# Row sums in buffers of their own, and half of the down projection's sums added by DVE, in a two-layer encoder step

## The chip, the core and the metric

The kernel runs on one core of a Trainium2 chip. The metric is the device time of one execution in microseconds (us). The median of three runs of the kernel before is 2804.59 us (2801.84 to 2804.91). Five engines are spoken of: PE (the matrix engine), DVE (the vector engine), ACT (the scalar engine), POOL (GpSimd, used here mostly to start DMAs that add into their target) and SP (which starts the other DMAs). Each works through its own instructions in program order and waits at an instruction until its inputs and its output buffer are ready. SBUF is the on-chip memory that all of them read. PSUM holds eight banks of 128 x 512 fp32 into which PE writes its sums.

## The reference, cut to what matters

The computation is one inference step of two layers over 640 tokens (512 of a prompt, 128 of running streams). Each layer has a half-step feed-forward part, a mixer and a second half-step feed-forward part, each followed by a layer norm. The change touches the feed-forward parts alone:

```python
D_MODEL = 1024
D_FF = 2816

def swiglu(x, w_gate, w_up, w_down):
    return (jax.nn.silu(x @ w_gate) * (x @ w_up)) @ w_down
...
x = layer_norm(ALPHA * x + 0.5 * swiglu(x, ffn_w_gate[l, 0], ffn_w_up[l, 0], ffn_w_down[l, 0]),
               ln_g[l, 0], ln_b[l, 0])
```

All values are fp32. There are four feed-forward parts, ffn0 to ffn3, with the mixers between them in the order ffn0, mix0, ffn1, ffn2, mix1, ffn3.

## The kernel before, in words

**Precision.** PE multiplies in a reduced fp32 format, so every operand is held as two parts, hi and lo. `split(hi, lo, src)` makes them: ACT copies the source into hi (L94), which rounds it, and DVE subtracts hi from the source into lo (L95). A product of two operands is three matmuls (hi x hi, lo x hi, hi x lo). Weights come by DMA into a `raw` buffer (four of them, 128 x 1024), and their parts go into a `w` buffer (six of them). The last operand of a matrix has a single buffer of its own, `w1`.

**Gate and up.** The 2816 hid channels are 22 tiles of 128, taken two at a time (`pair`). For one pair, the gate and the up projection are each a 2 x 2 block product done with seven products in place of eight. `matrix` runs the seven products in the order 1, 2, 6, 5, 7, 3, 4 (12 matmuls each, L355), and `operands` prepares the seven weight operands: products 1 and 2 use the weight itself, 6 and 5 use two sums that DVE builds in a buffer `sw` (L334) and that are then split into `w`, 7 and 3 use differences that DVE writes over the raw weight, and 4 uses `w1`. There is one `sw` buffer. DVE joins the products into the hid row `hf` (L400, L404, L407), the gate through `s` (L392, and ACT's silu at L394); ACT keeps some products in `mx` (L366). The hid rows are split into `h`, the left operands of the down projection.

**The down projection.** Four hid tiles at a time (two pairs) are multiplied with their rows of w_down and added to the running sum `yacc` (five token tiles, 0 to 4, of 128 x 1024). In ffn0 and ffn3 this is plain. In ffn1 and ffn2 four of the six down projections of a part go through `down7`, which applies the seven-product scheme to token tiles 0 to 3 as well. It takes the token tiles in two pairs, `tp` = 0 (tiles 0 and 1) and `tp` = 1 (tiles 2 and 3); tile 4 is added plainly by DVE (L501). The scheme needs sums and differences of the hid tiles: `row_sums`, called after the up matrix of each pair, has DVE write four of them (L439 to L442) into the `sw` buffer and split them into `hs`. It needs sums and differences of the weights too, which DVE writes over the raw weights (L459 to L462) and splits into `w` buffers (called T in the code). Then come the products 1, 2, 5, 6, 3, 7, 4 (L485), each for both token pairs. After each, `add` puts the PSUM bank into `yacc`: ACT scales the bank into an `ev` buffer (L492; there are three, 128 x 512), and a DMA started by POOL adds the buffer to `yacc` (L493). The same bank is used again by a later product, so PE must wait until it has been read.

**Order.** The down projection of the four tiles before is issued inside the first pair of the next four, between the gate matrix and the preparation of the up operands. A scheduler of the framework then sets the order on each engine from the program order and from when buffers come free. So two pairs and one `down7` make a period that repeats: gate, down7, up, row sums, gate, up, row sums. There are eight `down7` (four each in ffn1 and ffn2), 16 row sums and 112 adds.

Of the kernel before, what the change touches and what calls it, by code (L numbers as in the profile page):

```python
# [9 lines left out]
F32 = mybir.dt.float32  # L10
# [3 lines left out]
ALU = mybir.AluOpType  # L14
# [3 lines left out]
ALPHA = 4.0 ** 0.25  # L18
# [17 lines left out]
def kernel(ctx: ExitStack, tc: tile.TileContext, I, O, phases=PHASES):  # L36
    nc = tc.nc

    def pool(name, bufs=1, stack=ctx, **kw):
        return stack.enter_context(tc.tile_pool(name=name, bufs=bufs, **kw))  # L40
# [24 lines left out]
    def bank_a():  # L65
        return bank("a")

    def bank_b():
        return bank("b")
# [23 lines left out]
    def split(hi, lo, src):  # L93
        nc.scalar.copy(hi, src)  # L94
        return nc.vector.tensor_tensor(lo, src, hi.bitcast(F32), op=ALU.subtract)  # L95

    def raw_tile():
        return pools["raw"].tile([128, 1024], F32, name="raw")
# [4 lines left out]
    def two_units():  # L103
        return pools["w"].tile([128, 2, 2, 512], F32R, name="w")

    def split2(w, src):

        return split(w[:, :, 0], w[:, :, 1], src.rearrange("p (j c) -> p j c", j=2))
# [19 lines left out]
    def mm3(ps, lhs, rhs):  # L128
        n = 3 * len(lhs)
        k = 0  # L130
        for (wh, wl), (xh, xl) in zip(lhs, rhs):
            for a, b in ((wh, xh), (wl, xh), (wh, xl)):
                state["pe"] = nc.tensor.matmul(ps, a, b, start=(k == 0), stop=(k == n - 1)).ins  # L133
                k += 1
# [3 lines left out]
    yacc = act.tile([128, NT, D], F32, name="yacc")  # L138
# [72 lines left out]
    def ffn(i, ph, last, side=None):  # L211


        V = nc.vector
        Q = T // 2
        with ExitStack() as st:
            wk = pool(f"ffn{i}_wk", 1, st, reuse_waits="tile")
# [45 lines left out]
            for h in range(2):  # L263
                o, L = HALVES[h]
# [12 lines left out]
            for r in range(2):  # L277
                w = load_w(I["w_gate"][i, 2 + r])
                first[r] = g_row()
                for c in range(2):  # L280
                    p = bank_a()[:, :Q]
# [102 lines left out]
            def pair(f, before=None):  # L384
# [26 lines left out]
                for n, take in (("w_gate", gate), ("w_up", up)):  # L411
                    if n == "w_gate" and f == 2:
                        tick("gate")
                        continue
                    if n == "w_up" and before is not None:
                        down(before)
                    with tc.issue_after(state["acc0"]) if f == 2 else ExitStack():
                        A = operands(I[n][i, f], I[n][i, f + 1])
                    if n == "w_up":
                        for r in range(2):  # L420
                            ht[f + r] = h_tile()
                    matrix(A, take)
                    if n == "w_up" and ph in SEVEN and f < NF - 4:
                        row_sums(f)
                    tick("gate" if n == "w_gate" else "up")

            def by_pairs(t):

                return t[:, :TP].rearrange("p (n a c) -> p n a c", n=2, a=2)
# [3 lines left out]
            def row_sums(f):  # L433


                v = wk.tile([128, 1024], F32, name="sw", bufs=1)
                s1, s2, s3, s4 = (v[:, 256 * n:256 * n + 256].rearrange("p (n c) -> p n c", n=2) for n in range(4))
                p, q = by_pairs(hf[f]), by_pairs(hf[f + 1])
                V.tensor_tensor(s1, p[:, :, 1], q[:, :, 1], op=ALU.add)  # L439
                V.tensor_tensor(s2, s1, p[:, :, 0], op=ALU.subtract)  # L440
                V.tensor_tensor(s3, p[:, :, 0], p[:, :, 1], op=ALU.subtract)
                V.tensor_tensor(s4, q[:, :, 0], s2, op=ALU.subtract)  # L442
                o = hs[f] = wk.tile([128, 2, 1024], F32R, name="hs", bufs=2)
                split(o[:, 0], o[:, 1], v)

            def down7(fs):


                raws, direct = {}, {}
                for f in fs:  # L450
                    raws[f] = raw_tile()
                    nc.sync.dma_start(raws[f], I["w_down"][i, f])
                for f in fs:
                    direct[f] = two_units()
                    split2(direct[f], raws[f])

                for f in fs[::2]:
                    (b11, b12), (b21, b22) = ((r[:, :512], r[:, 512:]) for r in (raws[f], raws[f + 1]))
                    V.tensor_tensor(b22, b22, b12, op=ALU.subtract)  # L459
                    V.tensor_tensor(b12, b12, b11, op=ALU.subtract)  # L460
                    V.tensor_tensor(b11, b22, b11, op=ALU.add)
                    V.tensor_tensor(b21, b21, b11, op=ALU.subtract)  # L462
                T = {}
                for r in range(2):
                    for f in fs[::2]:
                        T[f + r] = two_units()
                        split2(T[f + r], raws[f + r])

                def left(f, p, tp):
                    tok = lambda k, a: ht[f + k][:, :, 256 * tp + 128 * a:256 * tp + 128 * a + 128]  # L470
                    if p in (1, 2, 4):
                        return tok(*{1: (0, 0), 2: (1, 0), 4: (1, 1)}[p])
                    o = 256 * {5: 0, 6: 1, 7: 2, 3: 3}[p] + 128 * tp
                    return hs[f][:, :, o:o + 128]

                def right(f, p):
                    return {1: direct[f][:, 0], 2: direct[f + 1][:, 0], 3: direct[f + 1][:, 1],
                            6: T[f][:, 0], 5: T[f][:, 1], 4: T[f + 1][:, 0], 7: T[f + 1][:, 1]}[p]

                def product(ps, tp, p, first):  # L480
                    n = 0
                    for f in fs[::2]:
                        a, b = left(f, p, tp), right(f, p)
                        for u, v in ((0, 0), (1, 0), (0, 1)):
                            nc.tensor.matmul(ps, a[:, u], b[:, v], start=(first and n == 0), stop=(n == 5),  # L485
                                             skip_group_check=True)
                            n += 1

                def add(ps, t, j):

                    e = wk.tile([128, 512], F32, name="ev", bufs=3)
                    nc.scalar.mul(e, ps, 0.5 / ALPHA)  # L492
                    nc.gpsimd.dma_start(yacc[:, t, 512 * j:512 * j + 512], e, accum_op=ALU.add)  # L493

                t = NT - 1
                for j in range(2):
                    pb = bank_a()
                    mm3(pb, [(ht[f][:, 0, t * 128:t * 128 + 128], ht[f][:, 1, t * 128:t * 128 + 128]) for f in fs],
                        [(direct[f][:, j, 0], direct[f][:, j, 1]) for f in fs])
                    ya = yacc[:, t, j * 512:j * 512 + 512]  # L500
                    state["acc"] = V.scalar_tensor_tensor(ya, pb, 0.5 / ALPHA, ya, op0=ALU.mult, op1=ALU.add).ins  # L501
                x, w = ([bank_b() for _ in range(2)] for _ in range(2))
                z = [bank_a() for _ in range(2)]
                for p, ps, a, j in ((1, x, 0, 0), (2, z, 0, 0), (5, w, 1, 1), (6, x, 0, 1), (3, w, 0, 1), (7, x, 1, 1),
                                    (4, x, 1, 0)):
                    for tp in range(2):
                        product(ps[tp], tp, p, p in (1, 2, 5))
                        add(ps[tp], 2 * tp + a, j)
# [1151 lines left out]
```

## Time and profile before

| what | value |
|---|---|
| median of three runs | 2804.59 us (2801.84 to 2804.91) |
| profiled execution, its own time | 2807.14 us |
| its span, first to last instruction | 2805.4 us |
| mean granted PE clock | 0.965 |
| ACT casts of row sums (hs) | 16, 1045 ns each |
| adds through ev | 112 on ACT, 596 ns each; 112 DMAs of 256 KB |

Views of the profile used below: busy time of each engine in chosen stretches with the clock that PE was granted (1.00 is full speed); the list of waits, each as who waited for whom, total us, times, longest us; and timelines, which give start and duration in us, the engine, the line, the operation, and in brackets the idle time before it and what ended it. A timeline row marked x24 is 24 instructions of the same kind in a run, and its duration reaches to the end of the last one; PE's matmuls overlap a little, so the distance from one start to the next is the better measure of its pace. PEld is PE's loading of weights. Durations of grouped instructions are in ns.

### The profile page before, as it was taken

The page shows a single profiled execution, that of the slowest core. Times are in us where ns is not written, and L with a number is a line of the kernel's source. Part 1 is how long each engine was busy: PE and PEld are TensorE (multiplying, and loading weights), DVE is VectorE, ACT ScalarE, POOL GpSimd, SP SyncE. Part 2 cuts the span into 40 slices and gives each one's busy share as a digit, 9 for nine tenths or more (in the row PEclk, how much of TensorE's full clock was granted, in tenths as well). Part 3 has the DMA queues.
Part 4 walks back from the last instruction along what each step waited for, and adds up shares of the span by engine and source line. Part 5 has one row for each costly group of instructions (what it writes and reads, how often), then busy time and mean ns, then how long its engine had stood idle before and what let it go on. Part 6 is the DMA issues. An engine that isn't in the chain of part 4 may idle for free. (4 is left out here: it accounts for less than half of the span.)

```text
span 2805.4 us, 40790 instructions
## 1 busy us (share of the span) xinstructions
PE 2597.0 (93%) x15577; PEld 2335.0 (83%) x15577; DVE 2021.5 (72%) x3654; ACT 1247.7 (44%) x2372; POOL 336.5 (12%) x468
## 2 busy tenths in 40 slices
PE   8999999999798888889988888999999999999998
PEld 8999998786488777779878777888999978988887
DVE  7788876758577557467866557677768688876767
ACT  4344443346343444444344444456646453433332
POOL 0000003000020110113010110231111133000001
PEclk9999999999799999999999999999999999999999
DMA  5233344432211542553142552635646552344442
GB/s 175 91 118 106 106 133 136 154 122 66 79 46 59 114 116 63 123 120 113 44 103 72 128 113 76 159 104 178 207 131 198 177 183 74 103 144 131 139 137 91
DMA packets 181875, 332.12 MB, mean 118 GB/s; under 512 B 20864, under 2 KB 91648, under 8 KB 181168
## 3 DMA queue, kind: packets, MB, share of 16 engines
q1 hardware_dynamic: 163792, 293.83, 32.9%
q0 software_dynamic: 17888, 35.69, 6.7%
q8 instruction: 122, 2.00, 0.3%
q14 instruction: 73, 0.60, 0.1%
HBM read 259.56 MB, written 40.54 MB: 107 GB/s over the span
## 5 line engine op out<-in xcount | busy, mean ns | idle before, releaser
L95 DVE TENSOR_TENSOR w<-raw,w 128x512 fp32r<-128x512 f32 (+1 forms) x617 | 539.0, 896 | 238.5 <-ACT w L94 236.2
L94 ACT CAST w<-raw 128x512 fp32r<-128x512 f32 (+1 forms) x617 | 453.1, 771 | 312.3 <-PE bank L133 114.4
L133 PE MATMUL bank<-xhi,w 128*128 128x256 f32 (+2 forms) x2528 | 556.5, 312 | 15.8 <-ACT xhi L94 8.2
L355 PE MATMUL bank<-T,w 128*128 128x320 f32 x2736 | 467.1, 327 | 90.2 <-ACT w L94 82.2
L355 PE MATMUL bank<-xhi,w 128*128 128x320 f32 x2432 | 541.6, 310 | 0.2 <-DVE w L95 0.2
L355 PEld LDWEIGHTS bank<-T,w 128*128 128x128 f32 x2736 | 438.9, 202 | 102.5 <-ACT w L94 86.4
L133 PEld LDWEIGHTS bank<-xhi,w 128*128 128x128 f32 x2528 | 422.6, 189 | 28.1 <-ACT xhi L94 9.1
L133 PE MATMUL bank<-w,h 128*128 128x512 f32 x1872 | 436.7, 391 | 0.7 <-DVE w L95 0.7
L355 PEld LDWEIGHTS bank<-xhi,w 128*128 128x128 f32 x2432 | 408.5, 188 | 6.9 <-issue 4.2
L133 PEld LDWEIGHTS bank<-w,h 128*128 128x128 f32 x1872 | 348.1, 188 | 76.3 <-issue 3.4
L133 PE MATMUL bank<-xlo,w 128*128 128x256 f32 (+2 forms) x1264 | 391.7, 310 | 3.8 <-DVE xlo L95 3.6
L355 PE MATMUL bank<-xlo,w 128*128 128x320 f32 x1216 | 375.7, 309 | 0.0
L133 PEld LDWEIGHTS bank<-xlo,w 128*128 128x128 f32 x1264 | 238.4, 189 | 6.1 <-DVE xlo L95 4.7
L355 PEld LDWEIGHTS bank<-xlo,w 128*128 128x128 f32 x1216 | 228.9, 188 | 0.0
L493 POOL DMA_DIRECT2D yacc<-ev x112 | 97.1, 911 | 810.4 <-ACT ev L492 501.4
L366 ACT COPY mx<-bank 128x320 f32<-128x320 f32 x228 | 97.0, 425 | 180.7 <-PE bank L355 180.0
L208 DVE SCALAR_TENSOR_TENSOR yacc<-bank,yacc 128x512 f32<-128x512 f32 x160 | 109.6, 687 | 80.0 <-PE bank L133 79.2
L95 DVE TENSOR_TENSOR w<-sw,w 128x1024 fp32r<-128x1024 f32 x76 | 93.0, 1223 | 60.7 <-ACT w L94 60.3
L400 DVE TENSOR_TENSOR hf<-bank,mx 128x320 f32<-128x320 f32 x120 | 58.6, 488 | 106.0 <-PE bank L355 100.7
L94 ACT CAST w<-sw 128x1024 fp32r<-128x1024 f32 x76 | 79.6, 1048 | 107.4 <-DVE sw L334 106.7
L492 ACT ACTIVATE ev<-bank 128x512 f32<-128x512 f32 x112 | 65.9, 596 | 129.7 <-DMA yacc<-ev 103.3
L485 PE MATMUL bank<-w,hs 128*128 128x512 f32 x384 | 96.3, 403 | 22.1 <-ACT ev L492 22.1
(415 smaller groups left out, 3351.6 us busy)
## 6 DMA issues: line engine op xcount, KB each, us to landing
raw<-in_w_gate_dram SPq DMA_DIRECT2D x88, 512.0 KB, 4.1
raw<-in_w_up_dram SPq DMA_DIRECT2D x88, 512.0 KB, 4.5
raw<-in_w_down_dram SPq DMA_DIRECT2D x88, 512.0 KB, 3.7
yacc<-ev POOLq DMA_DIRECT2D x112, 256.0 KB, 4.5
raw<-in_m_in_dram SPq DMA_DIRECT2D x52, 512.0 KB, 4.5
raw<-in_m_out_dram SPq DMA_DIRECT2D x24, 512.0 KB, 4.0
csb<-cs_d SPq DMA_DIRECT2D x20, 512.0 KB, 4.9
h<-in_ssd_h_dram SPq DMA_DIRECT2D x16, 512.0 KB, 5.9
```

Of the source, the lines that this page charges most:

```text
L94: nc.scalar.copy(hi, src)
L95: return nc.vector.tensor_tensor(lo, src, hi.bitcast(F32), op=ALU.subtract)
L133: state["pe"] = nc.tensor.matmul(ps, a, b, start=(k == 0), stop=(k == n - 1)).ins
L208: state["acc"] = nc.vector.scalar_tensor_tensor(ya, pb, scale, ya, op0=ALU.mult, op1=ALU.add).ins
L355: nc.tensor.matmul(ps, A[p][:, a, k * 128:k * 128 + 128], B[p][b][:, k, :], start=(first and n == 0), stop=(n == 11), skip_group_check=True)
L366: nc.scalar.copy(e[n], ps)
L400: V.tensor_tensor(t[:, c], ps, e, op=ALU.add)
L485: nc.tensor.matmul(ps, a[:, u], b[:, v], start=(first and n == 0), stop=(n == 5), skip_group_check=True)
L492: nc.scalar.mul(e, ps, 0.5 / ALPHA)
L493: nc.gpsimd.dma_start(yacc[:, t, 512 * j:512 * j + 512], e, accum_op=ALU.add)
```

## The change

Two edits are made. `row_sums` takes two `ev` buffers of 512 columns in place of the one `sw` buffer of 1024, and so splits them in two halves. In `down7`, `add` of token tiles 2 and 3 (`t // 2` is 1, the second token pair) is one DVE instruction from the PSUM bank to `yacc`; tiles 0 and 1 keep ACT, ev and the DMA. No buffer is added: `sw` stays for `operands` alone, and the three `ev` buffers serve both users.

```diff
             def row_sums(f):
 
 
-                v = wk.tile([128, 1024], F32, name="sw", bufs=1)
-                s1, s2, s3, s4 = (v[:, 256 * n:256 * n + 256].rearrange("p (n c) -> p n c", n=2) for n in range(4))
+                v = [wk.tile([128, 512], F32, name="ev", bufs=3) for _ in range(2)]
+                s1, s2, s3, s4 = (v[n // 2][:, n % 2 * 256:n % 2 * 256 + 256].rearrange("p (n c) -> p n c", n=2)
+                                  for n in range(4))
                 p, q = by_pairs(hf[f]), by_pairs(hf[f + 1])
...
                 o = hs[f] = wk.tile([128, 2, 1024], F32R, name="hs", bufs=2)
-                split(o[:, 0], o[:, 1], v)
+                for n in range(2):
+                    split(o[:, 0, 512 * n:512 * n + 512], o[:, 1, 512 * n:512 * n + 512], v[n])
...
                 def add(ps, t, j):
 
+                    if t // 2:
+                        ya = yacc[:, t, j * 512:j * 512 + 512]
+                        V.scalar_tensor_tensor(ya, ps, 0.5 / ALPHA, ya, op0=ALU.mult, op1=ALU.add)
+                        return
                     e = wk.tile([128, 512], F32, name="ev", bufs=3)
                     nc.scalar.mul(e, ps, 0.5 / ALPHA)
                     nc.gpsimd.dma_start(yacc[:, t, 512 * j:512 * j + 512], e, accum_op=ALU.add)
```

The scheduler answers with another order on DVE and ACT in ffn1 and ffn2; the parts outside these two keep theirs, as do POOL and SP but for the 56 DMAs that go. The first place is DVE's queue in ffn1 at the end of the up matrix of hid tiles 6 and 7 and the start of the gate matrix of tiles 8 and 9. Before, `sw` holds the row sums first and then the sums for the gate's products 6 and 5:

```order
L95 TENSOR_TENSOR h<-hf,h 128x640
L439 TENSOR_TENSOR sw<-hf 128x256
L95 TENSOR_TENSOR w_8976<-raw,w_8976 128x512
L95 TENSOR_TENSOR h<-hf,h 128x640
L440 TENSOR_TENSOR sw<-sw,hf 128x256
L442 TENSOR_TENSOR sw<-hf,sw 128x256
L392 TENSOR_TENSOR s<-bank,mx 128x320
L95 TENSOR_TENSOR hs<-sw,hs 128x1024
L334 TENSOR_TENSOR sw<-raw 128x512
L334 TENSOR_TENSOR sw<-sw,raw 128x512
L95 TENSOR_TENSOR w<-sw,w 128x2x512
```

After the change (lines past the first edit have moved by one) the gate's sums come at the start of the stretch, among the joins of the hid rows:

```order
L334 TENSOR_TENSOR sw<-raw 128x512
L400 TENSOR_TENSOR hf<-bank,mx 128x320
L334 TENSOR_TENSOR sw<-sw,raw 128x512
L95 TENSOR_TENSOR w<-sw,w 128x2x512
L334 TENSOR_TENSOR raw<-raw,sw 128x512
L334 TENSOR_TENSOR raw<-raw 128x512
L400 TENSOR_TENSOR hf<-bank,mx 128x320
```

The row sums come after eight other rows of the same queue, now in ev:

```order
L440 TENSOR_TENSOR ev<-hf 128x256
L442 TENSOR_TENSOR ev<-hf 128x256
L441 TENSOR_TENSOR ev<-ev,hf 128x256
L392 TENSOR_TENSOR s<-bank,mx 128x320
L443 TENSOR_TENSOR ev<-hf,ev 128x256
L95 TENSOR_TENSOR hs<-ev,hs 128x512
```

The sums for the gate's operands and their split stand ahead of the hid rows (hf) and the row sums, where they stood behind both. The second place is DVE's queue during the `down7` just before, from the plain adds of token tile 4 to the preparation of the up operands. Before:

```order
L501 SCALAR_TENSOR_TENSOR yacc<-bank,yacc 128x512 x2
L95 TENSOR_TENSOR w<-raw,w 128x2x512 x2
L95 TENSOR_TENSOR w_8840<-raw,w_8840 128x512
L95 TENSOR_TENSOR w<-raw,w 128x2x512
L334 TENSOR_TENSOR sw<-raw 128x512
L334 TENSOR_TENSOR sw<-sw,raw 128x512
L95 TENSOR_TENSOR w<-sw,w 128x2x512
L334 TENSOR_TENSOR raw<-raw,sw 128x512
L334 TENSOR_TENSOR raw<-raw 128x512
```

After (L495 is the new add on DVE, L507 the plain add that was L501):

```order
L507 SCALAR_TENSOR_TENSOR yacc<-bank,yacc 128x512 x2
L495 SCALAR_TENSOR_TENSOR yacc<-bank,yacc 128x512
L95 TENSOR_TENSOR w<-raw,w 128x2x512 x2
L495 SCALAR_TENSOR_TENSOR yacc<-bank,yacc 128x512
L95 TENSOR_TENSOR w_8832<-raw,w_8832 128x512
L495 SCALAR_TENSOR_TENSOR yacc<-bank,yacc 128x512 x2
L95 TENSOR_TENSOR w<-raw,w 128x2x512
L334 TENSOR_TENSOR sw<-raw 128x512
L334 TENSOR_TENSOR sw<-sw,raw 128x512
L495 SCALAR_TENSOR_TENSOR yacc<-bank,yacc 128x512
L95 TENSOR_TENSOR w<-sw,w 128x2x512
L334 TENSOR_TENSOR raw<-raw,sw 128x512
```

The adds stand between the splits of the difference weights (the first x2), the split of `w1` and the up operands. The sixth and the seventh add follow further down, each behind one more difference of the raw weight.

## The prediction

> **What bounds the kernel now.** I read the page first, then busy time and clock by stretches, then the waits, then the timelines around the two longest waits of the tensor engine (PE).
>
> ```profile
> PE 2597.0 (93%) x15577; PEld 2335.0 (83%) x15577; DVE 2021.5 (72%) x3654; ACT 1247.7 (44%) x2372; POOL 336.5 (12%) x468
> PE   8999999999798888889988888999999999999998
> PEclk9999999999799999999999999999999999999999
> ```
>
> PE is the bound overall, but its busy row dips in the middle slices, where ffn1 and ffn2 run. The stretches show more. The first six rows of this view are whole periods of ffn1 and ffn2 (two pairs of hid tiles and one seven-product down projection each, cut at the same point of the program); the last is a stretch of ffn0, which has neither row sums nor seven-product down projections.
>
> ```profile
> 945.20:1044.20 99.00, 82.17 (x444) 74.67 (x444) 60.12 (x83) 43.32 (x64) 12.16 (x15) 0.91 0.42 102
> ...
> 1667.60:1766.60 99.00, 82.85 (x444) 74.94 (x444) 60.03 (x83) 43.35 (x64) 12.10 (x15) 0.91 0.41 101
> sum 595.60, PE 494.08 PEld 447.81 DVE 360.09 ACT 259.57 POOL 72.73; mean PE 82.35 PEld 74.64 DVE 60.01 ACT 43.26 POOL 12.12
> 100.00:200.00 100.00, 99.42 (x589) 92.54 (x588) 85.39 (x211) 40.54 (x70) 6.77 (x3) 1.00 0.33 108
> ```
>
> The columns are PE, PEld, DVE, ACT, POOL, the granted clock and the DMA share. A period takes 595.6/6 = 99.3 us, with PE busy 82 us of it at a clock of 0.91; in ffn0 PE is busy 99.42 of 100 us at 1.00, beside a DVE that is busy 85.39. So PE loses time in ffn1 and ffn2. The waits say to whom:
>
> ```profile
> PE bank L355 <- ACT w L94: 82.2, 16, 5.2
> PE bank L485 <- ACT ev L492: 46.2, 26, 3.0
> ACT ev L492 <- DMA yacc<-ev: 103.3, 63, 5.6
> DVE w L95 <- ACT w L94: 296.5, 200, 11.6
> ```
>
> Sixteen waits of 5.1 us come after the sixteen row sums. One of them on PE, with the clean products before it:
>
> ```profile
> 949.50 0.45 PE L355 MATMUL bank<-xhi,w 128*128 128x320 f32 x2
> ...
> 953.01 3.74 PE L355 MATMUL bank<-T,w 128*128 128x320 f32 x24
> 956.59 0.45 PE L355 MATMUL bank<-xhi,w 128*128 128x320 f32 x2
> ...
> 961.86 0.46 PE L355 MATMUL bank<-xhi,w 128*128 128x320 f32 x2
> ...
> 970.67 0.90 PE L355 MATMUL bank<-T,w 128*128 128x320 f32 x2 [5.13 <-ACT w L94]
> 971.93 5.16 PE L355 MATMUL bank<-T,w 128*128 128x320 f32 x22 [0.36 <-DVE w L95]
> ...
> 976.93 0.45 PE L355 MATMUL bank<-xhi,w 128*128 128x320 f32 x2
> ```
>
> A matrix of seven products (84 matmuls) takes 961.86 - 949.50 = 12.36 us when nothing waits. At 961.86 the gate matrix of the next pair begins; after two products it needs the operand that is split from sw. That comes late, because sw still holds the row sums:
>
> ```profile
> 965.33 0.43 DVE L442 TENSOR_TENSOR sw<-hf,sw 128x256 f32<-128x256 f32 x1
> 966.87 1.23 DVE L95 TENSOR_TENSOR hs<-sw,hs 128x1024 fp32r<-128x1024 f32 x1 [0.71 <-ACT hs L94]
> 968.13 0.69 DVE L334 TENSOR_TENSOR sw<-raw 128x512 f32<-128x512 f32 x1
> 968.85 0.69 DVE L334 TENSOR_TENSOR sw<-sw,raw 128x512 f32<-128x512 f32 x1
> 969.58 1.04 ACT L94 CAST w<-sw 128x1024 fp32r<-128x1024 f32 x1 [2.37 <-DVE sw L334]
> 970.65 1.23 DVE L95 TENSOR_TENSOR w<-sw,w 128x1024 fp32r<-128x1024 f32 x1 [1.11 <-ACT w L94]
> ```
>
> The wait costs more than its length. The 24 matmuls after it span 970.67 to 976.93, 6.26 us, where the clean 24 from 953.01 to 956.59 took 3.58: 0.36 of the difference is a second wait, 2.3 us is a slower array. The clock rows show it:
>
> ```profile
> 955.00:965.00 10.00, 10.00 (x70) 10.00 (x70) 5.61 (x11) 3.16 (x6) 0.00 (x0) 1.00 0.17 32
> 970.60:974.00 3.40, 2.97 (x10) 2.57 (x11) 2.43 (x3) 0.90 (x2) 0.00 (x0) 0.50 0.00 0
> 977.00:983.00 6.00, 6.00 (x43) 6.00 (x42) 4.17 (x7) 3.02 (x6) 0.00 (x0) 1.00 0.21 77
> ```
>
> So one row sum costs 5.13 + 0.36 + 2.3 = 7.8 us. The other place is the down projection:
>
> ```profile
> 916.53 5.63 PE L133 MATMUL bank<-w,h 128*128 128x512 f32 x24
> 922.00 5.60 PE L485 MATMUL bank<-w,h 128*128 128x512 f32 x24
> 927.43 5.60 PE L485 MATMUL bank<-w,hs 128*128 128x512 f32 x24
> 935.21 3.05 PE L485 MATMUL bank<-w,hs 128*128 128x512 f32 x12 [2.17 <-ACT ev L492]
> 939.12 3.18 PE L485 MATMUL bank<-w,hs 128*128 128x512 f32 x12 [0.86 <-ACT ev L492]
> 945.20 4.45 PE L485 MATMUL bank<-w,h 128*128 128x512 f32 x12 [2.91 <-ACT ev L492]
> ```
>
> Clean, 24 matmuls of 512 columns take 927.43 - 916.53 = 10.90 us for 48, so 5.45. A product for one pair of token tiles (6 matmuls) is 1.36 us. Three waits of 5.9 us together are for ACT, which waits for a free ev buffer.
>
> **The change part by part.** *What PE needs without any wait.* A period is four matrices and 108 matmuls of 512 columns: 4 x 12.36 + 108/24 x 5.45 = 49.4 + 24.5 = 73.9 us. It takes 99.3, so 25.4 us per period are waits and slow clock. ffn1 and ffn2 have eight periods (112 adds of 14 each; 16 row sums at two each): 8 x 25.4 = 203 us. Row sums are 16 x 7.8 = 125 of that; the remaining 78 go to the eight down projections and smaller pieces.
>
> *Row sums in ev buffers.* The sums for the next gate matrix no longer wait for the row sums; the first fence on the order shows them issued ahead of the whole hid chain. The operand that came at 970.65 is then built during the up matrix. Removed: 125 us. Added: the split of hs in two halves. From the row of 1.23 us for 1024 columns and 0.69 for 512 (968.13, the same kind of two-operand instruction), that is 2 x 0.69 - 1.23 = 0.15 us of DVE a time, 0.3 per period, beside PE. Added too: s1 to s4 now wait until the accumulating DMAs have freed two ev buffers. Behind that wait on DVE stand the hs split and the splits of the next weights.
>
> ```profile
> L492 ACT ACTIVATE ev<-bank x112: 582/597/602, 923.6 to 1773.3; 128x512 f32<-128x512 f32 x112
> L493 POOL DMA_DIRECT2D yacc<-ev x112: 852/859/1226, 924.5 to 1774.1; - x112
> ...
> DMA to landing us min/median/max: 3.3/4.5/8.0
> ```
>
> ```profile
> L501 DVE SCALAR_TENSOR_TENSOR yacc<-bank,yacc x16: 679/683/689, 923.0 to 1746.0; 128x512 f32<-128x512 f32 x16
> ```
>
> The last DMA of a down projection is issued at its end, and the row sums come a 12.36 us matrix later. Even the slowest landing of 8.0 us is over by then, so I cost this wait at nothing; without that cover it is at most 8.0 us once per period.
>
> *Adds on DVE.* Seven of fourteen adds per down projection leave ACT (0.60 us each), POOL's queue (0.86) and the DMA. An ev buffer is held for 0.60 + 0.86 + 4.5 = 6.0 us, so three buffers let one add through every 2.0 us, while PE finishes a product every 1.36: that is the wait of today. With every second product on ACT they come every 2.7 us, and the ev wait goes. DVE gets 7 x 0.68 = 4.8 us per period. (The nearest row is the same instruction at L501.) DVE needs 60.0 + 4.8 + 0.3 = 65.1 us in a period of 73.9, which is 88%; ffn0 shows 85.39% beside a PE at 99.42. An exact 85.39% limit would make the period 76.2, 2.3 us more. That is the upper end for this cost; the lower is zero.
>
> *What is late next.* An add on DVE waits for its product on PE, and behind it in DVE's queue stand the splits of the difference weights (for products 7 and 4) and the operands of the next up matrix. I count from PE's first matmul of the down projection (t = 0): tile 4 to 5.45, then two token pairs of 1.36 us for each of products 1, 2, 5, 6, 3, 7, 4, so their ends are 8.2, 10.9, 13.6, 16.4, 19.1, 21.8 and 24.5. The splits for products 7 and 4 need weight buffers that product 1 frees at 8.2: a cast of 1.04 and two splits of 1.23 end at 11.7, and product 7 starts at 19.1. The up operands need buffers that product 6 frees at 16.4: cast and split 18.7, two differences 20.1, the add of product 3 20.8, the split from sw (cast ready at 21.1) 22.4; the up matrix wants it after two products, at 24.5 + 24/84 x 12.36 = 28.0. The tightest place is the last product: after one more difference (23.1) DVE adds product 7's second pair, which ends at 23.8, and PE wants that bank at 21.8 + 1.36 = 23.2. So PE may wait 0.6 us there, too little to slow the array much: the 12 matmuls behind the 0.86 us wait above took 3.18 us.
>
> *The sum.* Between 0 and 2.4 us per period stay; I take 1.2, half of the DVE limit, since both the count and the ffn0 row are nearer to no wait. Span 2805.4 - 203 + 10 = 2612. The profiled execution took 2807.1 and the median of the runs is 2804.6, 0.8 below the span, so the forecast is 2612.
>
> The 2.3 us of slow clock per wait and the shorter ones after the down projections are 25.4 minus the waits themselves (82.2 + 16 x 0.36 + 46.2 = 134 us, 16.8 per period), some 8.6 us per period, 69 us in all. The Trainium skill ("TensorE: Matmul & The Clock Gate", What's actually happening) says that an idle window of about 3.4 us halves the array's clock, with which the 0.50 above agrees, but also "For modeling, the ramp penalty is <1% of a typical kernel span". By that rule no more than 28 us of the 203 could be ramp, the gain would be 134 + 28 = 162, and the time 2653; the rows here say 2.5% of the span, and I go by them.
>
> **The rivals.**
> 1. *DVE becomes the bound.* For it: 88% busy in program order, and 1.11 us of waiting for ACT's cast at each split like the one at 970.65. Two of these in each of four matrices (8.9 us) and half a product (0.7 us) at each of seven adds (4.9) on top of 65.1 make 78.9 us per period, 5 more than PE: 40 us back, 2642. Against it: the new order puts other work into most of these gaps.
> 2. *The down projections still wait,* for DVE in place of ACT; only the row sums' 125 us go: 2680. For it: the adds stand among splits that wait for ACT. Against it: the margins counted above.
> 3. *The row sums' wait stays,* because the gate's operands now wait for something else, such as a weight buffer: 78 us go, 2727. Against it: the gate's buffers come free when the gate before is done.
> 4. *Slower.* DVE falls behind through the adds, and PE waits at the sw operand of all four matrices of a period as it does today at two, each at 7.8 us: 31.2 in place of 25.4, 46 us more, 2851. It decides once DVE needs more than today's 99.3 us per period; it needs 65.1 now.
> 5. *It does nothing,* as the row sums and adds were covered: about 2805. Against it: PE's wait rows name exactly ev and the operand from sw.
>
> **How the numbers follow.** My forecast has 0.70, rivals 1 to 5 have 0.10, 0.10, 0.05, 0.03 and 0.02. The forecast alone spans 2602 to 2621 (0 to 2.4 us per period). The range takes in rival 1 and a half-kept wait in the down projections (39 us over 2621): 2598 to 2660, with 0.5 us per period below for the reading of the clean period. Faster by over 0.2% (5.6 us, about what a measurement of this kernel tells from no change): 0.95; within: 0.02; slower: 0.03.
>
> **What would show it.** In the profile after, the sixteen 5 us waits of PE L355 for ACT's cast should be gone, the ev wait for DMA nearly so, PE at 98% or more and the clock at 0.99 or more in ffn1 and ffn2, and the period 74 to 76 us. I am wrong if PE waits there for DVE's adds, if DVE is over 95% busy in a period, or if 5 us waits stay.

## The result and the profile after

The changed kernel takes 2602.9 us (median of four runs, 2601.0 to 2604.5) against 2804.75 (four runs): a ratio of 0.9281, 95% interval 0.9265 to 0.9297. That is 202 us less, 197 to 206. The forecast was 2612 and its range 2598 to 2660.

Page of the changed kernel, the same rows as of before:

```profile
PE 2532.5 (97%) x15577; PEld 2294.5 (88%) x15577; DVE 2037.3 (78%) x3726; ACT 1214.9 (47%) x2332; POOL 285.8 (11%) x412
...
PE   9999999999969999999999999999999999999998
PEclk9999999999979999999999999999999999999999
```

The dip in the slices of ffn1 and ffn2 is gone; the one that is left (the twelfth slice, 716 to 781 us) lies in the mixer ahead of ffn1, outside the change. Two whole periods of ffn1, cut at the plain adds of token tile 4 (columns as in the prediction: PE, PEld, DVE, ACT, POOL, granted clock, DMA share):

```profile
908.62:982.39 73.77, 73.77 (x445) 69.27 (x444) 62.44 (x92) 39.13 (x59) 6.15 (x7) 1.00 0.41 111
982.39:1056.20 73.81, 73.81 (x445) 69.31 (x444) 62.17 (x92) 39.15 (x59) 6.06 (x7) 1.00 0.42 111
```

A period is 73.8 us where it was 99.3, PE is busy in all of it, and its clock is 1.00. The waits that answer to the four of before:

```profile
ACT ev L498 <- PE bank L487: 76.2, 40, 3.0
...
PE bank L355 <- ACT mx L366: 0.8, 3, 0.4
...
PEld bank L487 <- DVE yacc L495: 1.5, 8, 0.2
...
DVE w L95 <- ACT w L94: 141.5, 129, 7.1
```

The sixteen 5 us waits of PE's L355 for ACT's cast are gone: the row shown is the one that L355 has left in the list for PE's matmuls, and its longest wait is 0.4 us. ACT now waits for PE's products and no longer for a free ev buffer. No wait of PE's matmuls in the down projection is in the list. The only trace of the new adds on PE is 0.2 us of its weight load, once per down projection. DVE's own waits for ACT's casts, which rival 1 feared, have halved (296.5 us before).

The first place of the change, the end of the up matrix and the start of the next gate matrix (timeline; DVE and PE rows):

```profile
931.31 0.68 DVE L334 TENSOR_TENSOR sw<-sw,raw 128x512 f32<-128x512 f32 x1
932.03 1.05 ACT L94 CAST w<-sw 128x1024 fp32r<-128x1024 f32 x1 [2.56 <-DVE sw L334]
...
933.11 1.23 DVE L95 TENSOR_TENSOR w<-sw,w 128x1024 fp32r<-128x1024 f32 x1 [1.12 <-ACT w L94]
...
942.92 3.68 PE L355 MATMUL bank<-T,w 128*128 128x320 f32 x24
...
944.37 0.41 DVE L443 TENSOR_TENSOR ev<-hf,ev 128x256 f32<-128x256 f32 x1
944.74 0.69 DVE L95 TENSOR_TENSOR hs<-ev,hs 128x512 fp32r<-128x512 f32 x1
```

The operand from sw is split at 933.11 and done at 934.3. PE wants it at 942.92, 8.6 us later, and the row sums are still being written then. Before, PE stood at this point, and the same split came behind the row sums. The 24 matmuls take 3.68 us here.

The second place, the end of the down projection:

```profile
913.34 11.04 PE L487 MATMUL bank<-w,hs 128*128 128x512 f32 x48
924.22 1.52 PE L487 MATMUL bank<-w,h 128*128 128x512 f32 x6
925.73 1.67 PE L487 MATMUL bank<-w,h 128*128 128x512 f32 x6
```

Four products for both token pairs run without a break, and the last follows; before, three waits stood among these.

### The profile page after: what moved, and what is told of

The parts are those of the page before. It is cut to its first block, busy times and chain, and to the rows that moved or that the text cites. A ratio compares the mean times of both kernels' runs of the same rounds, so it can differ in the third digit from the quotient of the medians.

```text
span 2602.8 us, 40675 instructions
## 1 busy us (share of the span) xinstructions
PE 2532.5 (97%) x15577; PEld 2294.5 (88%) x15577; DVE 2037.3 (78%) x3726; ACT 1214.9 (47%) x2332; POOL 285.8 (11%) x412
## 5 line engine op out<-in xcount | busy, mean ns | idle before, releaser
L355 PE MATMUL bank<-xhi,w 128*128 128x320 f32 x2432 | 541.9, 310 | 0.7 <-ACT mx L366 0.4
L355 PE MATMUL bank<-T,w 128*128 128x320 f32 x2736 | 425.9, 309 | 0.4 <-ACT mx L366 0.4
L355 PEld LDWEIGHTS bank<-xhi,w 128*128 128x128 f32 x2432 | 406.0, 188 | 8.3 <-issue 4.4
L355 PEld LDWEIGHTS bank<-T,w 128*128 128x128 f32 x2736 | 406.3, 188 | 1.7 <-ACT mx L366 0.6
L355 PE MATMUL bank<-xlo,w 128*128 128x320 f32 x1216 | 375.0, 308 | 0.0
L355 PEld LDWEIGHTS bank<-xlo,w 128*128 128x128 f32 x1216 | 228.0, 188 | 0.3
L499 POOL DMA_DIRECT2D yacc<-ev x56 | 48.6, 902 | 652.1 <-ACT ev L498 597.9
L133 PE MATMUL bank<-w,og 128*128 128x512 f32 x432 | 106.3, 400 | 2.8 <-DVE og L1460 2.8
L133 PEld LDWEIGHTS bank<-w,og 128*128 128x128 f32 x432 | 80.6, 191 | 21.1 <-DVE og L1460 4.6
L394 ACT ACTIVATE s<-s 128x320 f32<-128x320 f32 x108 | 50.8, 471 | 88.4 <-DVE s L392 88.2
```

What stands on the lines that cost most here:

```text
L355: nc.tensor.matmul(ps, A[p][:, a, k * 128:k * 128 + 128], B[p][b][:, k, :], start=(first and n == 0), stop=(n == 11), skip_group_check=True)
L394: state["silu"] = nc.scalar.activation(t, ps, AF.Silu).ins
```

## The experiments

Each run is given as its ratio to the kernel before on the same chip, and as us on the scale of 2804.6.

**Row sums alone.** The edit of `row_sums` without that of `add`:

```diff
-                v = wk.tile([128, 1024], F32, name="sw", bufs=1)
+                v = [wk.tile([128, 512], F32, name="ev", bufs=3) for _ in range(2)]
...
-                split(o[:, 0], o[:, 1], v)
+                for n in range(2):
+                    split(o[:, 0, 512 * n:512 * n + 512], o[:, 1, 512 * n:512 * n + 512], v[n])
```

> Only the row sums move into two ev buffers; all fourteen adds of a down projection stay with ACT and the DMA. If the two edits remove two separate waits, as the prediction has it, the sixteen row-sum waits go at 7.8 us each (wait and slow clock) and the down projections keep theirs: 2805 - 125 = 2680 us. If the slow clock is worth little (a ramp under 1% of the span), a wait is worth its idle time of 5.5 us: 2805 - 88 = 2717 us or a little less. If one cause lies behind both kinds of wait, this edit alone gives either all (2603 us) or nothing (2805 us).

Ratio 0.9524 (0.9500 to 0.9547): 2671 us, 133 less (127 to 140). Two periods, and the two waits that stay:

```profile
929.41:1012.45 83.04, 77.95 (x445) 71.27 (x445) 58.91 (x85) 42.66 (x66) 12.16 (x15) 0.96 0.50 121
1012.45:1095.45 83.00, 77.06 (x444) 70.07 (x444) 58.68 (x85) 42.56 (x66) 12.16 (x15) 0.98 0.50 120
```

```profile
ACT ev L494 <- DMA yacc<-ev: 108.4, 62, 7.5
...
PE bank L487 <- ACT ev L494: 44.8, 26, 3.5
```

The list of PE's waits has no more L355 for ACT's cast of w, while the wait for ev is nearly as before (46.2). A period is 83.0 us: one down projection costs 83.0 - 73.8 = 9.2 us of waiting and slow clock.

**Adds alone.** The edit of `add` without that of `row_sums`:

```diff
                 def add(ps, t, j):
 
+                    if t // 2:
+                        ya = yacc[:, t, j * 512:j * 512 + 512]
+                        V.scalar_tensor_tensor(ya, ps, 0.5 / ALPHA, ya, op0=ALU.mult, op1=ALU.add)
+                        return
```

> Only the adds of token tiles 2 and 3 move to DVE; the row sums stay in sw. Two separate waits: the down projections' share of 78 us goes, 2727 us, and with the other edit alone the two savings add up to the whole of 202 us. Slow clock worth little: 46 us of idle time and some pieces, about 2755 us. One common cause: 2603 or 2805 us.

Ratio 0.9747 (0.9723 to 0.9771): 2734 us, 71 less (64 to 78). With the other edit that makes 204 us, against 202 for both at once, where each of the two savings is good to 7 us. So these are two separate waits, and the savings add.

```profile
964.31:1054.49 90.18, 79.20 (x444) 73.45 (x445) 64.17 (x90) 39.39 (x57) 6.09 (x7) 0.92 0.35 91
1054.49:1145.22 90.73, 79.74 (x445) 73.99 (x445) 64.24 (x90) 39.58 (x57) 6.06 (x7) 0.93 0.34 90
```

```profile
964.31 0.90 PE L355 MATMUL bank<-T,w 128*128 128x320 f32 x2 [5.13 <-ACT w L94]
965.57 5.87 PE L355 MATMUL bank<-T,w 128*128 128x320 f32 x22 [0.36 <-DVE w L95]
```

The 5.13 us wait is as it was, and the 22 matmuls behind it stay slow: 5.87 us, where the sixteen rows of the kernel before run from 4.58 to 6.04. A period is 90.5 us, so two row sums cost 16.7, or some 8.3 each.

**No accumulating DMA.** The DMAs behind the scaled ev buffers are left out, and with them the sums of token tiles 0 to 3:

```diff
                     e = wk.tile([128, 512], F32, name="ev", bufs=3)
                     nc.scalar.mul(e, ps, 0.5 / ALPHA)
-                    nc.gpsimd.dma_start(yacc[:, t, 512 * j:512 * j + 512], e, accum_op=ALU.add)
```

> The kernel before without the DMA behind each scaled ev buffer: the down projection's sums of token tiles 0 to 3 are scaled by ACT but never added to yacc (this part of the computation is left out). DVE gets no extra work and ACT keeps all of its own. If the buffers that the accumulating DMAs hold are the whole of the down projections' wait, this is as fast as the kernel with only the adds moved: 2727 us, and the DVE adds are free. If ACT's own work or queue is part of that wait, it stays above, towards 2805 us; if the DVE adds cost something, it comes out below the kernel with only the adds moved.

Ratio 0.9744 (0.9718 to 0.9771), 2733 us (2726 to 2741): the kernel with only the adds moved, to within 1 us. All 112 scalings stay on ACT here and DVE has nothing more to do. So what made PE wait was the time that the DMAs held the ev buffers, neither ACT's work nor its queue, and the seven DVE adds per down projection cost nothing that these runs can tell. More ev buffers, the other way to shorten that wait, were not tried.

**More work on PE.** Thirty needless matmuls in the wait behind the row sums (`warm` is set for the sixteen gate matrices that follow row sums):

```diff
                 take(0, 0, z, e[1])
+                if warm:
+                    d = bank_b()[:, :Q]
+                    for n in range(30):
+                        nc.tensor.matmul(d, A[2][:, 0, n % 4 * 128:n % 4 * 128 + 128], B[2][0][:, n % 4, :],
+                                         start=(n == 0), stop=(n == 29), skip_group_check=True)
                 product(x, A, 6, False)
```

> The kernel before with 30 needless matmuls of 320 columns (4.4 us) put on PE at each of the sixteen gate matrices that follow row sums, between its second and third product, into a PSUM bank that nobody reads. The wait for the operand from sw stays as long as it was, but PE is busy for most of it. If the array slows because PE stands idle, the 2.3 us of slow matmuls behind each wait go: 2805 - 16 x 2.3 = 2768 us, faster with more work. If the ramp is worth under 1% or the matmuls behind the wait are slow for another reason (DVE or DMA using the same memory), the time stays at 2805 us or rises.

Ratio 0.9915 (0.9891 to 0.9939): 24 us less (17 to 31) with 480 more matmuls. The place that was at 970.67 before:

```profile
961.93 0.46 PE L355 MATMUL bank<-xhi,w 128*128 128x320 f32 x2
...
965.45 4.56 PE L376 MATMUL bank<-xhi,w 128*128 128x320 f32 x30
970.75 0.56 PE L355 MATMUL bank<-T,w 128*128 128x320 f32 x2 [0.74 <-ACT w L94]
972.01 3.49 PE L355 MATMUL bank<-T,w 128*128 128x320 f32 x22 [0.70 <-DVE w L95]
975.33 0.64 PE L355 MATMUL bank<-xhi,w 128*128 128x320 f32 x2
```

```profile
970.70:974.00 3.30, 2.55 (x15) 2.29 (x16) 2.43 (x3) 0.81 (x1) 0.00 (x0) 1.00 0.00 0
```

```profile
PE bank L490 <- ACT ev L497: 49.7, 25, 3.4
```

Counted from the start of the gate matrix, the operand comes as late as before (8.8 us: 970.75 - 961.93, and 970.67 - 961.86), and the clock is 1.00 where it was 0.50. So the matmuls were slow because PE had stood idle.

It gives less than the 37 us expected, first because not all of the 2.3 us was slow clock. The first two of the 24 matmuls start 1.26 us ahead of the other 22 at each of the sixteen places, in both kernels, where two clean ones take 0.30 (3.58 / 12): they wait for the lo part that DVE makes, whatever the clock, and that wait costs 0.96 us and not 0.36. Only the 22 behind can gain. At this place they go from 5.00 us (976.93 - 971.93) to 3.32 (975.33 - 972.01), 1.7 less; over the sixteen places their rows fall from a mean of 5.35 us to 3.49, which makes 30 us. Second, the waits for ev in the down projections are 49.7 us where they were 46.2. That leaves 26 us, and 24 came.

**All adds on DVE.**

```diff
-                    if t // 2:
+                    if True:
```

> The changed kernel with all fourteen adds of a down projection on DVE, so that ACT, ev and the DMA have none. DVE was busy 62.3 of 73.8 us in a period of the changed kernel; seven more adds at 0.60 us from start to start make it 66.5, 90%. If PE stays the bound as long as DVE has any room, the time is the changed kernel's, 2603 us within 0.2%. If DVE must stay near the 85% that ffn0 shows, a period grows to 66.5 / 0.854 = 77.9 us, 4.1 more, and the kernel to 2636 us.

Ratio 0.9286 (0.9266 to 0.9307), 2604 us: no difference from the changed kernel (0.9281) that these runs can tell.

```profile
905.90:979.87 73.97, 73.79 (x445) 69.33 (x444) 66.70 (x100) 34.64 (x52) 0.00 (x0) 1.00 0.27 86
979.87:1054.04 74.17, 74.06 (x446) 69.56 (x445) 66.77 (x99) 34.66 (x52) 0.00 (x0) 1.00 0.27 86
```

DVE is busy 66.7 of 74.1 us, 90%, and PE still loses at most 0.4 us per period. DVE has no limit at 85% here.

**DVE overloaded.** One needless instruction behind each of these adds, then two (in the second expectation, "the kernel before" is the kernel with one):

```diff
                         V.scalar_tensor_tensor(ya, ps, 0.5 / ALPHA, ya, op0=ALU.mult, op1=ALU.add)
+                        V.tensor_tensor(ya, ya, ya, op=ALU.max)
```

> All adds on DVE, and behind each one needless instruction on DVE (the maximum of the sum with itself, 128 x 512, about 0.60 us from start to start). DVE then needs 66.5 + 8.4 = 74.9 us in a period, 101% of PE's 73.8. If PE's work sets the time until DVE is full, the least is 1.1 us per period, 9 us in all: 2612 us or a little over. If DVE's order costs PE waits that slow its clock, as the rival of a DVE bound has it, each matrix may lose some us: 1.1 + 4 x 2 us per period, about 2675 us.

> As the kernel before, with two needless instructions behind each add: DVE needs 83.3 us in a period against PE's 73.8. DVE must be the bound now: at least 9.5 us per period more, 76 us, 2679 us. With waits for ACT's casts (1.1 us at each of eight splits per period) and half a product at each of fourteen adds it would be nearer to 2679 + 8 x 18 = 2820 us. If DVE's time in a period is not what counts, it stays at 2603 us.

Ratios 0.9462 (0.9441 to 0.9483), 2654 us, and 0.9712 (0.9693 to 0.9732), 2724 us. Both lie between the least that DVE's busy time asks for and the dearer expectation. A period of each, the first with one instruction, the second with two:

```profile
1006.64:1085.88 79.24, 75.68 (x444) 69.33 (x444) 74.75 (x113) 35.00 (x52) 0.00 (x0) 1.00 0.25 80
```

```profile
1019.91:1108.63 88.72, 80.41 (x444) 72.69 (x444) 83.13 (x127) 35.06 (x52) 0.00 (x0) 0.94 0.23 72
```

And the waits of PE in the second:

```profile
PE bank L487 <- DVE yacc L495: 34.3, 26, 3.8
...
PE bank L355 <- ACT w L94: 27.3, 16, 3.5
```

DVE is busy 94% in both (74.75 of 79.24, 83.13 of 88.72): this is what a DVE bound looks like here. PE now waits at the places that the rivals named, the bank that DVE has to read and, for most of the second row's 27.3 us, the operand from sw. Even so the kernel with two needless instructions is still faster than the one before.

## Why the prediction was right, step by step

The forecast's mechanism held at every step; three terms were mis-sized, and the errors of two of them cancel.

*The clean period* was put at 73.9 us from rows of before and is 73.8. So 8 x 25.4 = 203 us were to be had, and 202 came.

*What stays* was the term that missed. I kept 10 us (1.2 per period); nothing stays. The term came from two steps. DVE's need was put at 65.1 us by adding up durations, but in a full queue most instructions start about 0.08 us before the last one's end, and the changed kernel shows 62.2 to 62.4. And ffn0's 85.39% was taken as a possible limit of DVE, though it only showed what DVE was asked to do there; with all adds on DVE it runs at 90% beside a PE that hardly waits.

*Row sums* were put at 125 us and measure 133 (127 to 140) alone. The 7.8 us per wait came from one wait; the rows behind the sixteen waits of the kernel before, of which these are the first and the last, run from 4.58 to 6.04 us and have a mean of 5.35, where the one I used had 5.16:

```profile
872.97 5.13 PE L355 MATMUL bank<-T,w 128*128 128x320 f32 x22 [0.36 <-DVE w L95]
...
1727.71 6.04 PE L355 MATMUL bank<-T,w 128*128 128x320 f32 x22 [0.44 <-DVE w L95]
```

That is 0.2 of the 0.5 us that was missing per row sum (8.3 against 7.8); for the other 0.3, 5 us in all, I have no row, and it lies within the interval of this run. How the 7.8 was split was wrong too: of its 2.3 us of slow matmuls, 0.6 were the longer wait for the lo part (0.96 in place of 0.36). The sum of the three pieces is the same.

*The down projections* were the remainder, 78 us, and so carry the same error with the other sign: 71 alone (64 to 78).

*Slow clock.* The rows gave 69 us to slow clock and small pieces. The single edits give nearly the same by another way: 133 + 71 us were saved where the printed waits were 88 and 46, so 70 us lie outside them. Some 10 of these are the part of the wait for lo that the row does not print (0.6 us at each of sixteen places), which leaves some 60 us, 2.1% of the span. That the idle time is the cause is shown for the row sums, by the kernel in which needless matmuls fill it; for the shorter waits of the down projection it is argued from the clock alone, which is 0.96 and 0.98 where only these waits are left. The rule of the Trainium skill ("TensorE: Matmul & The Clock Gate", What's actually happening) that the ramp is under 1% of a typical span would have given 2653 us; with 24 such places in one execution it does not hold here.

*What is late next.* The count put the end of the add of product 7 at t = 23.8 us and PE's need at 23.2, a wait of 0.6. In the trace, DVE and PE (its weight load) at this place:

```profile
924.99 0.68 DVE L495 SCALAR_TENSOR_TENSOR yacc<-bank,yacc 128x512 f32<-128x512 f32 x1
...
925.73 1.24 PEld L487 LDWEIGHTS bank<-w,h 128*128 128x128 f32 x6 [0.18 <-DVE yacc L495]
```

It is indeed the one place where PE's queue meets DVE, with 0.18 us on the weight load and none on the matmuls.

*The rivals.* That DVE becomes the bound, or that the down projections go on waiting for it, needs a DVE load that the change does not bring: the waits appear when DVE is asked for 101% of a period and not yet at 90%; between these nothing was tried. That the row sums' wait stays, or that both waits were covered and nothing changes, is excluded by the two single edits, with 133 and 71 us. The slower outcome was to begin at 99.3 us of DVE work per period; even 83.1 us leave the kernel at 2724 us, below the one before.

## What to carry to other kernels

A wait of the matrix engine cost its idle time and a slow stretch behind it: here 8.3 us where 5.5 were printed as waits, and even filling the wait with useless matmuls paid. When two uses share one buffer, the second waits for the whole life of the first; look for the wait whose releaser is a cast or a copy out of such a buffer, and give the off-path use another buffer that is idle at that moment. Moving work to the busiest side engine was free here up to 90% of the period, with an order that put each piece where it was due; add up its need from start to start, and judge it by the stretch in which it has to be done.

## What the runs showed of the hardware that was not expected

DVE at 90% of a period, with fourteen banks per down projection to clear on time, cost PE at most 0.4 us per period. At 101% the kernel lost 50 us (2654 against 2604), 6.3 per period and some six times the 1.1 us by which the work was reckoned to be too much. That the overload lies within the down projection, where all the added instructions stand, is a likely reason; no run separates it.

A printed wait can be shorter than what it costs. Behind the row sums, the two matmuls that ran ahead of the wait for lo took 0.90 us at the slow clock and 0.56 at the full one, and the rows gave the wait as 0.36 and 0.70; the 1.26 us from the first matmul to the third were the same.
